# Strassen's seven products for the first two gate/up blocks, one step per token quarter

## The chip, the cores and the metric

The kernel runs on one NeuronCore of a Trainium2 chip. TensorE (PE) multiplies matrices; VectorE (DVE), ScalarE (ACT) and GpSimd (POOL) do elementwise work; SyncE (SP) issues most transfers. Each engine has its own instruction stream, which it executes in order, and semaphores tie the streams together. The metric is the device time of one execution in microseconds (us).

## The reference, cut to what matters

1024 prompt tokens and 64 sample tokens, model width 1024, fp32, one layer:

```python
h = rmsnorm(x, g_mix); z = h @ w_in                    # 1024 -> 5 * 512
b_gate, c_gate, v, glu_val, glu_gate = split(z, 5)
y_a = b_gate * dwconv3(c_gate * v)
y_b = silu(layernorm(dwconv31(glu_val * sigmoid(glu_gate)) + bias))
x = x + concat(y_a, y_b) @ w_out                       # "out projection"
h2 = rmsnorm(x, g_ffn)                                 # "second norm"
x = x + (silu(h2 @ w_gate) * (h2 @ w_up)) @ w_down     # d_ff = 2816 = 22 blocks of 128
y = rmsnorm(x, g_final)
```

The sample tokens have their own convolution histories, and the new histories are outputs too.

## The kernel before, in words

Activations stand transposed, channels on partitions, tokens along the columns. The 1088 columns are two halves of 544, and four pieces of 272. A *quarter* `s` (0 or 1) here is the piece `s` of each half, so 2 x 272 columns (`quarter`). Every matmul is 128x128 by 272 columns, in fp16. An fp32 product is made of three of them: each operand is split into a high fp16 part (a copy on ACT, `high`, L312) and a low one (the rest, on DVE, `low`, L315), and high x high, high x low and low x high are added in PSUM (`products`, L299). Weights are split the same way when they are loaded (`split_w`, L275 on ACT and L276 on DVE), into eight slots of 512 columns (`whl`), or, if an entry is marked resident, into a tile of its own.

From the third block on, gate and up of a block are one Strassen step. The weights of the block form a 2x2 (rows of the model's halves, columns gate and up), the operands another (B11, B12, B21, B22: half of the model width by half of the tokens), and seven products replace eight (`SEVEN`). They need sums of weights (S1 to S4, on POOL, L501 to L512) and differences of operands (T1 to T4, on DVE). The first two blocks are plain (`plain_task`): for each quarter, block, and gate or up, one task of 8 x 3 x 2 = 48 matmuls. They run while the operands of the Strassen steps come to be: quarter 0's norm (`second_norm`) during quarter 1's out projection, its differences (`combinations`) from that one's end on, and quarter 1's both during the plain tasks.

What sets the order is a list of tasks, written out in program order (`run_tasks`). A task is one group of matmuls, what reads its banks (`post`), and some steps of background work (`bg`): the layer norm, the second norm or the differences, each a generator of which a `Stream` takes so many steps. At the start of a task the low halves that were left over are issued (`flush`, over the list `late`), and up to two weight tiles are prepared (`fill_one`), at most 12 tasks ahead and only while one of the eight slots is free; a resident one only from the out projection on. Each engine's queue follows that order. Column sums of a norm go to PE in the middle of another task, at a share of its matmuls (`midway`, PART1 to PART3). Accumulators are pairs of PSUM banks, three of them in this stage, taken in turn (`bank2`). Small scratch tiles (`small`) are a pool of eleven.

The out projection runs quarter 0 (L1103 adds its result to x), then quarter 1. For quarter 0 its first three blocks are each cut in two: part a takes the terms of the first three channel blocks, part b the rest. Those three blocks' weights are split again for quarter 1.

Transfers of weights go through two tiles `wf` of 1 MB on SP's queue; preparing the first entry of a load issues the next load, which waits until the tile's last reader is done.

After the plain tasks `begin_strassen` cuts the banks anew and hands the operands of blocks 0 and 1 for the down product to `late`, where each waits a number of turns (`delayed`).

Of the kernel before, what the change touches and what calls it, by code (L numbers as in the profile page):

```python
# [132 lines left out]
NPART, NBEG = 3, 3  # L133

ORDER1 = (*range(NPART, KB), *range(NPART))
LASTG = len(GROUPS) - 1
# [26 lines left out]
def trunk(ctx, tc, x, par, sta, stb, w_in, w_o, w_gu, w_ds, w_dl, y, st_out):  # L163
# [60 lines left out]
    def bank2():  # L224
        k = psum["turns"][psum["n"] % len(psum["turns"])]
        psum["n"] += 1
# [56 lines left out]
    def products(outs, terms, first=True, last=True, part=(0, None), low_last=None):  # L283
# [3 lines left out]
        if low_last:  # L287
            todo.sort(key=lambda a: a[1] == low_last)
        one, end = todo[0], todo[-1]
        todo = todo[slice(*part)]  # L290
# [112 lines left out]
    for s, b in [(0, b) for b in range(KB)] + [(1, b) for b in ORDER1]:  # L403
        if b >= NPART and s:
            W_O[s, b] = W_O[0, b]
            continue
        if b % 2 == 0 or s and b == NPART:
            raws.append((w_o[b // 2], 2048, s == 0 and b < 2 * (NPART // 2 + 1)))
        r, o, e = len(raws) - 1, (b % 2) * 1024, len(entries)
        if b < NPART:  # L410
            W_O[s, b] = [(e + q, 0) for q in range(2)]
            entries += [dict(raw=r, off=o + WS * q, n=WS) for q in range(2)]
        else:
            W_O[s, b] = [(e, q * WS) for q in range(2)]
            entries.append(dict(raw=r, off=o, n=1024, resident=True))
    W_GU, W_DN = {}, {}

    def gate_up_entries(n):
        W_GU[n] = len(entries)
        if n < NE:  # L420
            entries.extend(dict(raw=len(raws), off=WS * q, n=WS) for q in range(4))
        else:
            entries.extend(dict(raw=len(raws), strassen=a[0], n=WS) for a in SEVEN)
        raws.append((w_gu[n], 2048, False))

# [11 lines left out]
    for n in range(GROUPS[0][1]):  # L437
        gate_up_entries(n)
# [24 lines left out]
    def prepare(i):  # L463
# [15 lines left out]
        if name is None:  # L479
            o, n = e["off"], e["n"]  # L480
            return split_w(raw[:, o : o + n], e.get("resident") and unit_v, raws[r][2])
# [17 lines left out]
        if name == "S1":  # L499
# [3 lines left out]
            sums["S2"] = s2  # L503
            src = s1
        elif name == "S2":
            src = sums["S2"]
# [3 lines left out]
        elif name == "S4":  # L510
            src = sums["S2"]
# [21 lines left out]
    def fill_one(t, first=None):  # L533
# [5 lines left out]
        if res and t < marks["out"] or not res and len(live) == NSLOT:  # L539
            return False  # L540
# [441 lines left out]
    def b_post(acc, j, hf):  # L982
# [9 lines left out]

        return rest
# [78 lines left out]
    def out_task(b, s, *bg, part=None):  # L1072
        ws = W_O[s, b]

        def terms(ks):
            out = []
            for k in ks:
                w, col = ws[k // NJ]
                t = (ya + yb)[k]
                out.append((whl[w], col + (k % NJ) * P, [(t, s * CW), (t, HT + s * CW)]))  # L1080
            return out

        def emit_a():
            keep["out", b] = bank2()
            pair_products(keep["out", b], terms(range(NBEG)), last=False)

        def emit_b():
            while s not in ln_done:
                flush()
                ln(1)  # L1090
            flush()
            acc = keep.pop(("out", b))
            pair_products(acc, terms(range(NBEG, KB)), first=False)
            return acc

        def emit():
            acc = bank2()
            pair_products(acc, terms(range(KB)))
# [7 lines left out]
        w = sorted({w for w, _ in ws})  # L1106
        if part == "a":
            add(w[:1], emit_a, lambda _: None, *bg)
        elif part == "b":
            add(w, emit_b, post, *bg)  # L1110
        else:
            add(w, emit, post, *bg)

    ssum, rstd2 = {}, {}
# [794 lines left out]
```

## Time and profile before

| | |
|---|---|
| median of 3 runs | 1001.45 us (1001.19 to 1001.87) |
| profiled execution | 1001.27 us |
| its span, first to last instruction | 999.5 us |
| granted TensorE clock | 0.999 |
| PE, DVE, ACT, POOL busy | 987.7, 721.9, 421.5, 358.0 us |
| matmuls | 8664 |

A row of a timeline reads: start, duration, engine, line of the kernel, operation, what is written <- what is read, shapes, count, and in brackets how long the engine was idle before it and what ended that. A matmul's duration contains its pipeline, so the pace is read from the distance of starts. In a row of stages each engine has its busy time and, in brackets, its instructions; then come the granted clock (1.00 is full), the share of the transfer engines and GB/s.

### The profile page before, as it was taken

To read this page: it belongs to the slowest core of one execution; us is meant where nothing else is said; L and a number is where in the kernel's file an instruction comes from. 1 tells how busy PE (TensorE), PEld (TensorE's weight loads), DVE (VectorE), ACT (ScalarE), POOL (GpSimd) and SP (SyncE) were. 2 spreads that over 40 slices of the span, in tenths; PEclk is the share of its full clock that TensorE was granted. 3 is DMA by queue.
4 is the path that set the end of the run, shared out by engine and by line. 5 is a ranking of instruction groups with operands and counts; after the bars stand their busy time and mean duration, and the time that the engine had idled before them with its cause. 6 is when DMAs were issued, how large, how long until landed. Compare 5 with 4: busy or idle time off the path is not lost.

```text
span 999.5 us, 20038 instructions
## 1 busy us (share of the span) xinstructions
PE 987.7 (99%) x8664; PEld 835.9 (84%) x8664; DVE 721.9 (72%) x1009; ACT 421.5 (42%) x742; POOL 358.0 (36%) x295
## 2 busy tenths in 40 slices
PE   8999999999999999999999999999999999999997
PEld 8888888888888888888888888888888888888886
DVE  6959999987676778866665665666566556676586
ACT  6512243247452534644223444422345443244455
POOL 1947986656000204232134212213422221363044
PEclk9999999999999999999999999999999999999999
DMA  9300111111500111120112112111211201131105
GB/s 341 110 19 25 61 44 54 43 43 58 209 1 1 43 43 44 43 74 33 65 43 85 43 43 75 33 64 43 86 44 43 75 33 64 65 127 43 43 2 179
DMA packets 18568, 64.61 MB, mean 65 GB/s; under 512 B 1296, under 2 KB 9632, under 8 KB 13616
## 3 DMA queue, kind: packets, MB, share of 16 engines
q1 hardware_dynamic: 18160, 63.12, 18.1%
q8 instruction: 67, 1.10, 0.4%
q14 instruction: 21, 0.17, 0.1%
q10 hardware_dynamic: 272, 0.13, 0.0%
q0 software_dynamic: 48, 0.09, 0.0%
HBM read 58.28 MB, written 5.05 MB: 63 GB/s over the span
## 4 chain that ended last, share of the span: by engine, by line
PE 76%; DVE 19%; issue 2%; ACT 2%; POOL 1%; DMA 1%; DVEq 0%; SPq 0%; ACTq 0%; POOLq 0%
PE two L299 69%; DVE cv L641 12%; PE one L817 3%; PE one L1651 1%; DVE u L315 1%; DVE whl L276 1%; PE one L299 1%; PE stat L324 1%; DVE v L1167 1%; PE two L1651 1%; DMA u<-w_in 1%; DVE cv L636 1%; DVE s L985 0%; DVE u L956 0%; ACT h L312 0%
## 5 line engine op out<-in xcount | busy, mean ns | idle before, releaser
L299 PEld LDWEIGHTS <-whl 128*128 128x128 f16 x7182 | 702.7, 98 | 131.7 <-issue 2.2
L299 PE MATMUL two<-u,whl 128*128 128x272 f16 x4416 | 523.3, 279 | 0.5 <-DVE u L315 0.3
L299 PE MATMUL two<-h,whl 128*128 128x272 f16 x2736 | 329.5, 279 | 0.8 <-DVE s L985 0.6
L512 POOL TENSOR_TENSOR s<-wf,s 128x512 f32<-128x512 f32 (+1 forms) x32 | 37.7, 1177 | 397.9 <-DVE whl L276 397.9
L641 DVE SCALAR_TENSOR_TENSOR cv<-u,par_t,cv 128x1024 f32<-128x1024 f32 x108 | 130.6, 1303 | 0.1
L1373 DVE SCALAR_TENSOR_TENSOR s<-two,s 128x544 f32<-128x544 f32 x60 | 43.5, 724 | 108.9 <-PE two L299 108.9
L276 DVE SCALAR_TENSOR_TENSOR whl<-wf,whl 128x512 f16<-128x512 f32 (+1 forms) x150 | 116.3, 781 | 3.8 <-ACT whl L275 3.8
L275 ACT ACTIVATE whl<-wf 128x512 f16<-128x512 f32 (+1 forms) x150 | 87.1, 586 | 73.1 <-PE two L299 71.6
L1487 DVE SCALAR_TENSOR_TENSOR xt<-two,xt 128x544 f32<-128x544 f32 x84 | 60.8, 724 | 55.9 <-PE two L299 55.6
L275 ACT ACTIVATE whl<-s 128x512 f16<-128x512 f32 (+1 forms) x96 | 56.1, 584 | 67.1 <-PE two L299 60.9
L276 DVE SCALAR_TENSOR_TENSOR whl<-s,whl 128x512 f16<-128x512 f32 (+1 forms) x96 | 62.2, 652 | 19.9 <-ACT whl L275 19.5
L501 POOL TENSOR_TENSOR s<-wf 128x512 f32<-128x512 f32 (+1 forms) x32 | 39.4, 1232 | 93.7 <-DVE s L356 91.7
L299 PE MATMUL two<-u,v 128*128 128x272 f16 x480 | 56.3, 279 | 0.0
L312 ACT ACTIVATE h<-s 128x544 f16<-128x544 f32 (+2 forms) x62 | 37.9, 623 | 40.3 <-DVE s L1416 11.4
L1369 ACT ACTIVATE s<-two 128x544 f32<-128x544 f32 x60 | 36.9, 614 | 42.8 <-PE two L299 42.6
L299 PEld LDWEIGHTS <-v 128*128 128x128 f16 x480 | 47.0, 98 | 9.0
L274 POOL TENSOR_TENSOR whl<-wf,whl 128x512 f16<-128x512 f32 x38 | 46.9, 1259 | 10.1 <-ACT whl L273 10.1
L817 PE MATMUL one<-h,u 128*128 128x272 f16 (+2 forms) x480 | 46.1, 256 | 1.0 <-ACT h L312 1.0
L817 PEld LDWEIGHTS <-u 128*128 128x128 f16 x480 | 39.9, 98 | 7.2 <-issue 1.4
L508 POOL TENSOR_TENSOR wf<-wf 128x512 f32<-128x512 f32 (+1 forms) x32 | 43.8, 1369 | 0.0
L315 DVE TENSOR_TENSOR h<-s,h 128x544 f16<-128x544 f32 (+2 forms) x61 | 40.6, 687 | 3.0 <-ACT h L312 1.9
L502 POOL TENSOR_TENSOR s<-s,wf 128x512 f32<-128x512 f32 (+1 forms) x32 | 41.4, 1294 | 2.5
(167 smaller groups left out, 801.8 us busy)
## 6 DMA issues: line engine op xcount, KB each, us to landing
wf<-w_gu SPq DMA_DIRECT2D x22, 1024.0 KB, 4.9
wf<-w_ds SPq DMA_DIRECT2D x12, 768.0 KB, 4.1
wf<-w_in SPq DMA_DIRECT2D x8, 1024.0 KB, 5.1
wf<-w_o SPq DMA_DIRECT2D x6, 1024.0 KB, 5.0
xt<-x SPq DMA_DIRECT2D x3, 1088.0 KB, 12.5
y<-xt SPq DMA_DIRECT2D x4, 544.0 KB, 3.4
u<-w_in SPq DMA_DIRECT2D x4, 512.0 KB, 7.5
wf<-w_dl SPq DMA_DIRECT2D x2, 1024.0 KB, 4.9
```

Source lines behind the costliest of these rows:

```text
L274: return whl, lambda: gps.tensor_tensor(lo, wf, hi, ALU.subtract) and None
L275: act.activation(hi, wf, AF.Copy, scale=WSC)
L276: return whl, lambda: dve.scalar_tensor_tensor(lo, wf, WSC, hi, ALU.mult, ALU.subtract) and None
L299: pe.matmul(out, w_[:, wpart, col : col + P], hl[:, apart, t0 : t0 + out.shape[1]], start=first and (i, q) == one, stop=last and (i, q) == ...
L315: eng.tensor_tensor(lo, tmp, hi, ALU.subtract)
L501: gps.tensor_tensor(s1, a21, a22, ALU.add)
L502: gps.tensor_tensor(s2, s1, a11, ALU.subtract)
L508: gps.tensor_tensor(a21, a11, a21, ALU.subtract)
L641: dve.scalar_tensor_tensor(o_, i_, w, c, ALU.mult, ALU.add)
L817: pe.matmul(accs[c, i][:, o : o + cw], w4[i][:, wpart, k * P : (k + 1) * P], h[k][:, apart, t0 : t0 + cw], start=len(done) == 1, stop=len( ...
L1373: dve.scalar_tensor_tensor(o, src, IN_SC, o, ALU.mult, ALU.add)
L1487: dve.scalar_tensor_tensor(o, bk[a_][:, :, :CW], IN_SC, o, ALU.mult, ALU.add)
```

## The change

Blocks 0 and 1 become Strassen steps too, both in one task, one token quarter at a time: seven tasks per quarter, each of 2 blocks x 12 matmuls of one 272-column piece (`duo_tasks`). The order of the seven products differs between the quarters (`DUO`); in quarter 1 the last product has a bank of its own and is joined by DVE. The results are kept by half, both blocks in one tile (`gate`).

The second norm makes operands per quarter, each name in a tile of its own, in the order in which the products use them (`FORMS`), with the differences made in place. B12, which no product uses, is not made. `STEPS0` and `DUO_STEPS` say how many steps run in each task: all of quarter 0's run in quarter 1's out projection.

The weights of the two blocks are prepared in the order of use, block 0 and 1 in turn: A11 and A12 as one resident tile of 1024 columns, S1 and S2 resident, S3, S4 and A22 in slots. `since` says from which task after the out projection's start a resident entry may be prepared. Both blocks' loads stay in `wf` until A22 is split.

The out projection is no longer cut: eight tasks per quarter. Block 0 takes the fourth channel block last (`K_FIRST`), and that one's last low half is issued at once. The weights of its first three blocks stay in six slots for quarter 1. The layer norm's steps for quarter 1 begin in the first out task and not in the fourth.

The down product's operands of blocks 0 and 1 wait 5, 10, 15 and 20 turns in `late` (`BEHIND`), not 0, 3, 6 and 9.

```diff
-NPART, NBEG = 3, 3
+NPART = 3
 ORDER1 = (*range(NPART, KB), *range(NPART))
+FORMS = ("T1 T2 B21 T3 B22 T4".split(), "T1 B21 T2 B22 T3 T4".split())
+K_FIRST = 0, 1, 2, 4, 5, 6, 7, 3
+BEHIND = 5
+STEPS0 = (1, 2, 2, 2, 2, 3, 3, 100)
+DUO = ("A11 S1 S2 A12 S3 S4 A22", "A11 S1 A12 S2 S4 S3 A22")
+DUO_STEPS = ((1, 0, 2, 2, 2, 1, 2), (1, 2, 2, 2, 2, 100, 0))
...
+    def bank2(k=None):
+        if k is None:
+            k = psum["turns"][psum["n"] % len(psum["turns"])]
+            psum["n"] += 1
...
-    def products(outs, terms, first=True, last=True, part=(0, None), low_last=None):
...
         for n, (i, q) in enumerate(todo):
-            for part_, fn in list(midway):
+            for part_, fn in list(midway) if beside else ():
...
-    for s, b in [(0, b) for b in range(KB)] + [(1, b) for b in ORDER1]:
...
-        if b % 2 == 0 or s and b == NPART:
-            raws.append((w_o[b // 2], 2048, s == 0 and b < 2 * (NPART // 2 + 1)))
+    for b in range(KB):
+        if b % 2 == 0:
+            raws.append((w_o[b // 2], 2048, b < 2 * (NPART // 2 + 1)))
...
+    def first_pair_entries():
+        r = len(raws)
+        raws.extend((w_gu[n], 2048, False) for n in range(NE))
+        W_GU.update((n, {}) for n in range(NE))
+        for what, since in (("A", 5), ("S1", 9), ("S2", 9), ("S3", 0), ("S4", 0), ("A22", 0)):
+            for n in range(NE):
+                e = len(entries)
+                if what == "A":
+                    W_GU[n].update(A11=(e, 0), A12=(e, WS))
+                    entries.append(dict(raw=r + n, off=0, n=2 * WS, resident=n, since=since + n))
+                    continue
+                W_GU[n][what] = e, 0
+                entries.append(dict(raw=r + n, strassen=what, n=WS))
+                if what in ("S1", "S2"):
+                    entries[-1].update(resident=n, since=since)
...
+            home = None
+            if "resident" in e:
+                home = unit if e["resident"] is not True and e["resident"] == 0 else unit_v
...
+        if "resident" in e:
+            if name == "S1":
+                sums["two", r] = unit_v([P, 2, 2, n], F16)
+            return split_w(src, lambda *_: sums["two", r][:, "S1 S2".split().index(name)])
         return split_w(src)
...
-        if res and t < marks["out"] or not res and len(live) == NSLOT:
+        if res and t < marks["out"] + entries[i].get("since", 0):
+            return False
+        if not res and len(live) == NSLOT:
             return False
...
+        if (j, hf) == (NJ - 1, 1):
+            return rest()
         return rest
...
-    def out_task(b, s, *bg, part=None):
...
+        def emit():
+            assert s in ln_done
+            acc = bank2()
+            terms = []
+            for k in K_FIRST if b == 0 else range(KB):
...
+                terms.append((whl[w], col + (k % NJ) * P, [(t, s * CW), (t, HT + s * CW)]))
+            pair_products(acc, terms)
             return acc
...
-        w = sorted({w for w, _ in ws})
-        if part == "a":
-            add(w[:1], emit_a, lambda _: None, *bg)
-        elif part == "b":
-            add(w, emit_b, post, *bg)
...
+    def operand(name, kp, s):
+        return ops[name, s].rearrange("p a k c -> p a (k c)"), kp * CW
...
+        tq, ts, pend = {}, {}, []
+        def settle(n):
+            while len(pend) > n:
+                low(*pend.pop(0))
+        def put(name, u, t):
+            if (name, s) not in ops:
+                ops[name, s] = unit([P, 2, 4, CW], F16)
+            o = ops[name, s][:, :, 2 * u : 2 * u + 2]
+            high(o[:, 0], t)
+            pend.append((o[:, 1], t, o[:, 0]))
+            settle(1)
+        def norm(u, q):
+            new = unit if (s, u, q) == (0, 0, 0) else single_v if (u, q) == (1, 1) else unit_v
+            t = tq[u, q] = new([P, 2, 2, CW])
+            for kk in range(2):
+                k = 4 * q + 2 * u + kk
+                dve.scalar_tensor_tensor(
+                    t[:, kk], quarter(xt[:, k], s), prm(PG2 + k), r, ALU.mult, ALU.mult
+                )
+        def form(name, u):
+            if name[0] == "B":
+                t = tq[u, int(name[1]) - 1][:, :, int(name[2]) - 1]
+            else:
+                b11, b12, b21, b22 = (tq.get((u, q), tq[u, 0])[:, :, i] for q in (0, 1) for i in (0, 1))
+                if name == "T1":
+                    ts[u] = halves(small())
+                a, b, t = {
+                    "T1": (b12, b11, ts[u]),
+                    "T2": (b22, ts[u], ts[u]),
+                    "T3": (b22, b12, b12),
+                    "T4": (b21, ts[u], ts[u]),
+                }[name]
+                dve.tensor_tensor(t, a, b, ALU.subtract)
+            put(name, u, t)
...
+            norm(u, 0)
+            form("B11", u)
+            yield
+        for name in FORMS[s]:
+            for u in range(2):
+                if name == FORMS[s][1]:
+                    norm(u, 1)
+                    yield
+            for u in range(2):
+                form(name, u)
                 yield
         settle(0)
         yield
...
-    def plain_task(n, q, s, *bg):
...
+    def copied(src):
+        o = halves(small())
+        act.activation(o, src, AF.Copy, scale=IN_SC)
+        return o
+    def joined(src, o):
+        dve.scalar_tensor_tensor(o, src, IN_SC, o, ALU.mult, ALU.add)
+        return o
+    def duo_tasks(s):
+        bk = {}
+        order = DUO[s].split()
+        chained = order[-2] != "S3"
+        seven = {w_: (b_, a_) for w_, b_, a_ in SEVEN}
+        if not chained:
+            seven["A22"] = "T4", "W"
+        homes = {"Y": "ab"[s], "Z": "a", "W": "ba"[s]}
+        def gate(hf, src, by, sg):
+            if hf not in fu:
+                fu[hf] = unit([P, NE, HT])
+            o = fu[hf][:, :, s * CW : (s + 1) * CW]
+            dve.scalar_tensor_tensor(o, src, by, sg, ALU.mult, ALU.mult)
+        def task(i):
+            name = order[i]
+            b_, a_ = seven[name]
+            fresh = a_ not in [seven[w_][1] for w_ in order[:i]] or not chained and name == "A22"
+            final = a_ not in [seven[w_][1] for w_ in order[i + 1 :]] or not chained and name == "A12"
+            def emit():
+                if a_ not in bk:
+                    bk[a_] = bank2(homes[a_])
+                for n in range(NE):
+                    w, col = W_GU[n][name]
+                    terms = [
+                        (whl[w], col + kp * P, [operand(b_, kp, s)]) for kp in range(4)
+                    ]
+                    products([bk[a_][:, n, :CW]], terms, fresh, final, beside=n == 1)
+            def post(_):
+                acc = bk[a_][:, :, :CW]
+                if name == "A11":
+                    bk["c11"] = copied(acc)
+                elif name == "S1":
+                    bk["c22"] = copied(acc)
+                elif name == "S2":
+                    bk["c12"] = copied(acc)
+                elif name == "A12":
+                    sg = joined(acc, bk["c11"])
+                    act.activation(sg, sg, AF.Silu)
+                elif name == "S3":
+                    joined(acc, bk["c22"])
+                    if not chained:
+                        bk["c21"] = copied(acc)
+                elif name == "S4":
+                    sg = joined(acc, bk["c12"])
+                    act.activation(sg, sg, AF.Silu)
+                elif chained:
+                    gate(0, acc, 1.0 / WSC, bk["c11"])
+                else:
+                    gate(0, joined(acc, bk["c21"]), ASC, bk["c11"])
+                if name == order[5]:
+                    return lambda: gate(1, bk["c22"], ASC, bk["c12"])
+            add([W_GU[n][name][0] for n in range(NE)], emit, post, lambda: step_on(s, i))
+        for i in range(7):
+            task(i)
+    def step_on(s, i):
+        if s == 0 and i == 0:
+            sn[0](100)
+        sn[1](DUO_STEPS[s][i])
...
-                    return f_done(n, hf, fu[n][:, hf * HT : (hf + 1) * HT])
-                late.append(lambda k=3 * (2 * n + 1 - hf), fn=start: delayed(k, fn))
+                    return f_done(n, hf, fu[hf][:, n])
+                late.append(lambda k=BEHIND * (2 * n + 2 - hf), fn=start: delayed(k, fn))
...
-                    hl, c0 = operand(b_, kp)
-                    terms.append((whl[w], kp * P, [(hl, c0), (hl, c0 + CW)]))
+                    terms.append((whl[w], kp * P, [operand(b_, kp, s) for s in range(2)]))
...
-    comb = [Stream(combinations(s)) for s in range(2)]
...
-    for b in range(NPART):
-        out_task(b, 0, lambda: ln(1) if 0 not in ln_done else None, part="a")
...
         def bg(b=b):
-            if b >= NPART:
-                ln(1 if b < KB - 1 else 100)
+            ln(1 if b < KB - 1 else 100)
...
-        out_task(b, 0, bg, part="b" if b < NPART else None)
+        out_task(b, 0, bg)
...
+        out_task(b, 1, lambda i=i: sn[0](STEPS0[i]))
     for s in range(2):
-        for n in range(NE):
...
-                plain_task(n, q, s, bg)
+        duo_tasks(s)
```

More of the change, by code (lines that the diff above doesn't have):

```diff
@@ L436, in trunk @@
     aside = set()
-    for n in range(GROUPS[0][1]):
+    first_pair_entries()
+    for n in range(NE, GROUPS[0][1]):
         gate_up_entries(n)
@@ L510, in prepare @@
         elif name == "S4":
-            src = sums["S2"]
+            src = sums["S2", r]
             gps.tensor_tensor(src, a12, src, ALU.subtract)
```

142 lines of the change are left out of this document (12 added, 130 removed).

## The prediction

> **What bounds the kernel now.** I read the busy shares and the chain that ended last first.
>
> ```profile
> span 999.5 us, 20038 instructions
> PE 987.7 (99%) x8664; PEld 835.9 (84%) x8664; DVE 721.9 (72%) x1009; ACT 421.5 (42%) x742; POOL 358.0 (36%) x295
> PE 76%; DVE 19%; issue 2%; ACT 2%; POOL 1%; DMA 1%; DVEq 0%; SPq 0%; ACTq 0%; POOLq 0%
> ```
>
> PE is busy all the time and 76% of the chain is its own. The DVE part of the chain is early (the taps) and around the stage that the change rewrites, so the second view is the stages there: the out projection of quarter 1 (first row), the plain gate/up blocks (second), the first Strassen block (third).
>
> ```profile
> core 0: us, PE busy (x) PEld busy (x) DVE busy (x) ACT busy (x) POOL busy (x), PEclk, DMA share, GB/s
> 296.20:335.10 38.90, 38.90 (x338) 32.86 (x337) 27.42 (x41) 14.29 (x24) 0.00 (x0) 1.00 0.01 1
> 335.10:381.40 46.30, 45.88 (x391) 38.30 (x389) 36.13 (x55) 20.51 (x34) 7.50 (x5) 1.00 0.13 46
> 381.40:400.00 18.60, 18.60 (x163) 15.70 (x162) 15.88 (x18) 8.05 (x15) 9.97 (x7) 1.00 0.16 58
> ```
>
> The clock is full (1.00), PE has no gap to speak of, and DVE runs at 70%, 78% and 85%. So matmuls taken out are time taken out, as long as DVE, which makes the operands, keeps up. Third view, the timeline of PE, then of DVE, in that stage:
>
> ```profile
> 295.57 22.87 PE L299 MATMUL two<-u,v 128*128 128x272 f16 x196
> 318.27 21.94 PE L299 MATMUL two<-u,whl 128*128 128x272 f16 x188
> ...
> 340.31 0.76 PEld L324 LDWEIGHTS stat<-s,ones 128*128 128x128 f32 x4 [0.39 <-DVE s L356]
> 340.31 1.18 PE L324 MATMUL stat<-s,ones 128*128 128x272 f32 x4
> 341.33 19.04 PE L299 MATMUL two<-u,whl 128*128 128x272 f16 x163
> 360.69 59.54 PE L299 MATMUL two<-u,whl 128*128 128x272 f16 x510 [0.32 <-DVE u L315]
> ...
> 960.06 4.33 PE L299 MATMUL one<-h,u 128*128 128x272 f16 x36
> 964.23 2.25 PE L299 MATMUL one<-h,whl 128*128 128x272 f16 x18
> ```
>
> From 295.57 to 318.27, 196 matmuls take 22.70 us: 0.1158 us each. In the last two rows, where a weight tile serves one matmul and not two, 36 take 4.17 us: 0.1158 again. PE waits for DVE twice: 0.39 us ahead of the column sums, 0.32 us for a low half.
>
> ```profile
> 329.59 0.73 DVE L1103 SCALAR_TENSOR_TENSOR xt<-two,xt 128x544 f32<-128x544 f32 x1 [2.06 <-PE two L299]
> 330.23 0.72 DVE L1188 TENSOR_TENSOR s<-v,s 128x544 f32<-128x544 f32 x1
> 330.86 0.72 DVE L315 TENSOR_TENSOR u<-s,u 128x544 f16<-128x544 f32 x1
> ...
> 335.15 0.72 DVE L1103 SCALAR_TENSOR_TENSOR xt<-two,xt 128x544 f32<-128x544 f32 x1 [0.46 <-PE two L299]
> ...
> 338.33 1.29 DVE L276 SCALAR_TENSOR_TENSOR whl<-wf,whl 128x512 f16<-128x512 f32 x2
> 339.53 0.72 DVE L356 TENSOR_TENSOR s<-s,s 128x544 f32<-128x544 f32 x1
> ...
> 381.39 0.72 DVE L1336 SCALAR_TENSOR_TENSOR u<-two,s 128x544 f32<-128x544 f32 x1 [1.64 <-PE two L299]
> ```
>
> The rows at 335.15 and 381.39 start on PE's last matmul of the out projection and of the plain blocks: the stage lasts 46.24 us. Tasks of 48 matmuls are 5.56 us apart (329.59, 335.15). One DVE instruction of 544 columns follows another after 0.64 us; the low half of a 512-column weight tile takes 0.60.
>
> **The change, part by part.** *Strassen for blocks 0 and 1.* Plain: 8 tasks of 48 matmuls = 384. Strassen: 2 quarters x 7 products x 2 blocks x 12 = 336. Each at 0.1158, and the column sums at 0.92 (a distance below): the stage should be 384 x 0.1158 + 0.92 = 45.39 and is 46.24, so 0.85 us of it is waiting. The new one without waits is 336 x 0.1158 + 0.92 = 39.83 us: 6.41 less than now, 5.56 of it matmuls. PE's weight loads stay one per matmul and shorter than it.
>
> *DVE's account.* I count from the end of the out projection (0). Norms and newton steps from these rows:
>
> ```profile
> 294.65 1.08 PE L324 MATMUL stat<-s,ones 128*128 128x272 f32 x4
> 295.57 22.87 PE L299 MATMUL two<-u,v 128*128 128x272 f16 x196
> ...
> 296.87 0.72 DVE L344 SCALAR_TENSOR_TENSOR stat<-stat,s 128x544 f32<-128x544 f32 x1
> 299.16 1.47 DVE L1167 SCALAR_TENSOR_TENSOR u<-xt,par_t,stat 128x544 f32<-128x544 f32 x2
> ...
> 302.43 1.47 DVE L1167 SCALAR_TENSOR_TENSOR v<-xt,par_t,stat 128x544 f32<-128x544 f32 x2
> 303.81 1.35 DVE L315 TENSOR_TENSOR u<-u,u 128x544 f16<-128x544 f32 x2
> ...
> 341.59 0.62 ACT L341 ACTIVATE s<-stat 128x544 f32<-128x544 f32 x1 [2.02 <-PE stat L324]
> 342.23 1.28 ACT L1333 ACT_TABLE_LOAD   x1
> 343.52 0.62 ACT L1333 ACTIVATE s<-two 128x544 f32<-128x544 f32 x1
> ```
>
> Three newton steps are 2.29, a pair of norms 1.38. Quarter 0's combinations all move into the out projection: per task xt and the square's add 1.28, plus 1.9 to 3.8 of norms, differences and low halves, plus 1.2 for two weight tiles: 3.8 to 5.2 us of each 5.56. They fit, barely; nothing on PE waits until the queue is over a task late, as there are three pairs of banks. If that cover goes, the lateness arrives at the column sums.
>
> There, DVE has xt, T4's last difference, two low halves, two weight tiles and the add: 6 x 0.64 + 1.2, with 0.15 for a copy on ACT about 5 at worst, 4.7 as I lay it out; PE gets there at 47 matmuls, 5.44. Slack 0.5 to 0.7, where today PE waits 0.39. The sums end at 6.4, the root on ACT at 7.1, newton at 9.4. Then in order of use, with the joins and gates between them (0.64 each): B11's low halves by 15.3 (PE wants them at 20.4), T1's by 21.9 (23.2), B21's by 25.2 (25.9), T2's by 27.1 (28.7), B22's by 30.7 (31.5), T3's by 33.2 (34.3), T4's by 35.8 (37.1). Every operand is early, but by 0.7 to 1.6 us; DVE is busy some 34 of 39.8 us, 86%. ACT's table load (1.28), today right behind the root, comes ahead of quarter 0's first silu and holds T1's copies to 15.9 and 16.5, just as DVE asks for them. The bank that quarter 0's last product leaves is read at 23.3, while the second quarter asks for one at 23.2: 0.1. So I bound the new waits by 0 and by the 0.85 of today for a likely course, and take 0.4.
>
> *Weights.* The four splits per block become an unsplit pair (1024 wide), and S1, S2, S3, S4, A22; six re-made splits of the out weights and their two 1 MB loads go. DVE loses 6 + 8 low halves of 0.60 and gets ten, and two wide ones:
>
> ```profile
> 249.21 2.35 DVE L276 SCALAR_TENSOR_TENSOR v<-wf,v 128x1024 f16<-128x1024 f32 x2
> ```
>
> 8.4 us against 6.0 + 2.4, the same. SP's load of block 2 now waits until block 0's A22 is split, at 3.4:
>
> ```profile
> wf<-w_gu SPq DMA_DIRECT2D x22, 1024.0 KB, 4.9
> ```
>
> It lands at 8.3; ACT wants it at 7.6 and holds only a copy behind it until B11's high half at 10.8. On SP only block 3's load is queued behind. Cost 0; if it were 3 us later ACT's copies would follow, still ahead of 20.4.
>
> *Out projection without its split first three blocks, layer norm three tasks sooner, last low half at once.* PE's work is the same. Block 0 wants ya3 after 42 matmuls, 4.9 us in; its low half, behind one DVE instruction and one copy of 0.64, is done some 2 us in. Where layer norm's second half runs today, PE has no gap:
>
> ```profile
> 268.00:296.20 28.20, 28.20 (x234) 23.54 (x233) 18.79 (x29) 16.67 (x23) 0.00 (x0) 1.00 0.11 38
> ```
>
> So a sooner one gains 0; it loses at most what one blocked DVE instruction costs (1.7, below), as its chain from sums to sums is the same. I take 0.
>
> *POOL.* S1 to S4 of two blocks are eight more instructions. What one costs DVE:
>
> ```profile
> 340.39 2.90 POOL L501 TENSOR_TENSOR s<-wf 128x512 f32<-128x512 f32 x1 [91.68 <-DVE s L356]
> ...
> 344.59 1.27 POOL L508 TENSOR_TENSOR wf<-wf 128x512 f32<-128x512 f32 x1
> 344.72 1.71 DVE L315 TENSOR_TENSOR u<-s,u 128x544 f16<-128x544 f32 x1 [2.56 <-ACT u L312]
> ...
> 395.99 1.72 POOL L508 TENSOR_TENSOR wf<-wf 128x512 f32<-128x512 f32 x1
> 396.50 0.71 DVE L1373 SCALAR_TENSOR_TENSOR s<-two,s 128x544 f32<-128x544 f32 x1
> ```
>
> A low half that meets one takes 1.71 for 0.72, so 1.0 us is lost; an instruction that reads a PSUM bank (L1373) loses nothing. Six of the eight need only block 0's and 1's loads and a free scratch tile, and POOL is idle: they should run in the middle of the first out quarter, where DVE has gaps. Block 2's three meet newton and norms, which read PSUM. So I take 0, with 12 x 1.0 as the upper bound.
>
> This split by operand is also what the Trainium skill says (SBUF — State Buffer, "Who interferes with whom"): a VectorE instruction with two SBUF inputs contends with a GpSimd one that reads SBUF, and the later one blocks fully. The trace agrees (1.71 against 0.71). By that rule alone all low halves and differences that overlap would pay, which is the second rival.
>
> *Blocks 0 and 1's operands for the down product* come up to 20 queue turns later, not 9. The third row of stages (85% DVE) gets lighter at first: 0, as PE waits for nothing there today.
>
> **Sum.** The profiled execution took 1001.27 us, 1.8 around its span, against a median of 1001.45. 1001.27 - 6.41 + 0.4 = 995.3.
>
> **Rivals.** *First, DVE sets the pace in the new stage.* If block 2's three POOL instructions meet low halves (3 x 1.0) and two copies on ACT are exposed (0.6 each, like the silu above), T1 and B21 are 4.2 late against 0.7 of slack: 3.5 of waits, 998.4. For it: 86% with slacks under 2 us. Against: what is late once is then early for the rest, as PE moves back too.
>
> *Second, slower: POOL's port.* All twelve POOL instructions fall between the last out tasks and quarter 1's T1, and each holds a two-input DVE instruction up by 1.0: 12 - 0.7 = 11.3 us, 1006.2. It decides from the eighth on, when 6.41 + 0.7 is used up. For it: today POOL waited 91.7 us for a scratch tile until 340.39, just there. Against: the scratch tiles which the eight get were freed tasks earlier.
>
> *Third, no gain: weights late.* Six of eight slots are held to the end of the stage, so block 2 begins with two tiles. Were two of its tasks 2.78 us late each, 5.56 is lost: 1000.4. For it: DVE at 85% there. Against: the third tile is asked for five tasks after the first slot is freed.
>
> **How the numbers follow.** Forecast 0.62 (994.5 to 996.5), first rival 0.21 (to 999.3), third 0.09, second 0.08. A measurement of this kernel tells about 0.2%, 2 us, from no change. Faster by more takes the forecast and nearly all of the first: 0.82; same 0.10; slower 0.08. Low is 994.86 less the scatter of the runs, 994.5; reaching into the first rival until some 8 in 10 are held gives 998.6.
>
> **What would show it.** Right: 48 matmuls fewer, the stage near 40 us, PE's wait ahead of the sums gone, waits on low halves together under 1 us, POOL's new rows before the last out tasks. Wrong: a PE wait of over 1 us on L315 or on a gate, DVE rows of 1.7 us in a row ahead of it, or PE waiting for weight tiles in block 2.

## The result, and the profile after

The changed kernel takes 995.49 us (median of 6 executions, 994.87 to 995.70), the kernel before, in the same session, 1001.32 us (1000.68 to 1002.10). The ratio is 0.9940, with a 95% interval of 0.9928 to 0.9953. It is faster by 5.8 us, or 0.6%, and the forecast was 995.3 us. One later execution of the changed kernel took 1282.6 us at a mean clock of 0.752 and is left out of its median below. The page of the changed kernel, in the rows that answer to those of before:

```profile
span 993.7 us, 19954 instructions
PE 982.2 (99%) x8616; PEld 831.8 (84%) x8616; DVE 729.7 (73%) x1010; ACT 423.3 (43%) x743; POOL 369.8 (37%) x303
PE 78%; DVE 16%; issue 2%; ACT 1%; POOL 1%; DMA 1%; DVEq 0%; SPq 0%; ACTq 0%; POOLq 0%
```

There are 48 matmuls fewer, PE's busy time is down by 5.5 us and the span by 5.8. DVE and POOL have 8 and 12 us more to do, and it does not show in PE's time. The timeline of PE through the new stage (line numbers are those of the changed kernel; L309 is `products`):

```profile
318.20 16.84 PE L309 MATMUL two<-u,whl 128*128 128x272 f16 x144
334.88 1.55 PE L309 MATMUL two<-u,u 128*128 128x272 f16 x12
336.27 4.22 PE L309 MATMUL two<-u,v 128*128 128x272 f16 x35
340.33 1.08 PE L334 MATMUL stat<-s,ones 128*128 128x272 f32 x4
...
346.92 5.72 PE L309 MATMUL two<-u,whl 128*128 128x272 f16 x48
353.31 2.94 PE L309 MATMUL two<-u,whl 128*128 128x272 f16 x24 [0.67 <-DVE s L1335]
...
363.04 4.33 PE L309 MATMUL two<-u,v 128*128 128x272 f16 x36
367.21 73.02 PE L309 MATMUL two<-u,whl 128*128 128x272 f16 x629
```

The stage begins at 334.88 with A11 of block 0. Quarter 1's last three products begin at 367.21, and with 72 matmuls of 0.1158 they end at 375.55: 40.67 us, against 46.24 before. Without waits it would be 39.83, so 0.84 is waiting. That is what it was before (0.85), at another place: the waits for the column sums and for a low half are gone, and there is one ahead of the 24 matmuls of quarter 0's A22. The row's 0.67 counts from the modelled end of the last matmul; by the distance of starts it is 353.31 - (346.92 + 48 x 0.1158) = 0.83, which is all the waiting that the stage has. What PE waits for stands on DVE:

```profile
342.16 0.73 DVE L354 SCALAR_TENSOR_TENSOR stat<-stat,s 128x544 f32<-128x544 f32 x1 [2.19 <-ACT s L351]
...
344.46 2.86 DVE L1175 SCALAR_TENSOR_TENSOR v<-xt,par_t,stat 128x544 f32<-128x544 f32 x4
347.24 1.01 DVE L325 TENSOR_TENSOR u<-v,u 128x544 f16<-128x544 f32 x1
...
351.31 0.71 DVE L325 TENSOR_TENSOR u<-s,u 128x544 f16<-128x544 f32 x1
351.94 0.68 DVE L289 SCALAR_TENSOR_TENSOR whl<-s,whl 128x512 f16<-128x512 f32 x1
352.55 0.71 DVE L1335 SCALAR_TENSOR_TENSOR s<-two,s 128x544 f32<-128x544 f32 x1
353.18 2.84 DVE L1175 SCALAR_TENSOR_TENSOR v<-xt,par_t,stat 128x544 f32<-128x544 f32 x4
```

From 342.16 on DVE has no gap: newton, four norms, a low half, weights, the join of A12 (348.77), T1's steps, weights, and at 352.55 the join that reads S3's sum out of its bank pair (L1335, `joined`). In quarter 0, A11, S2, S3 and A22 all add up in that one pair, so A22 may not write there before the join has read it. POOL's new instructions ran here:

```profile
266.67 1.28 POOL L526 TENSOR_TENSOR s<-wf 128x512 f32<-128x512 f32 x1 [18.09 <-DMA wf<-w_gu]
...
277.98 3.47 POOL L533 TENSOR_TENSOR wf<-wf 128x512 f32<-128x512 f32 x2
311.54 3.52 POOL L537 TENSOR_TENSOR s<-wf,s 128x512 f32<-128x512 f32 x2 [30.09 <-DVE v L289]
343.81 1.27 POOL L526 TENSOR_TENSOR s<-wf 128x512 f32<-128x512 f32 x1 [28.74 <-DVE stat L355]
```

Six of the eight are in the first out quarter, two (S4) in the second; block 2's three come at 343.81, beside newton and the norms.

### The profile page after: what moved, and what is told of

It reads as the page before. It is cut to its first block, busy times and chain, and to the rows that moved or that the text cites. A ratio compares the mean times of both kernels' runs of the same rounds, so it can differ in the third digit from the quotient of the medians.

```text
span 993.7 us, 19954 instructions
## 1 busy us (share of the span) xinstructions
PE 982.2 (99%) x8616; PEld 831.8 (84%) x8616; DVE 729.7 (73%) x1010; ACT 423.3 (43%) x743; POOL 369.8 (37%) x303
## 4 chain that ended last, share of the span: by engine, by line
PE 78%; DVE 16%; issue 2%; ACT 1%; POOL 1%; DMA 1%; DVEq 0%; SPq 0%; ACTq 0%; POOLq 0%
PE two L309 72%; DVE cv L672 12%; PE one L848 3%; PE one L1680 1%; PE one L309 1%; PE two L1680 1%; PE stat L334 1%; DVE cv L667 1%; DMA u<-w_in 1%; DVE s L1016 0%; DVE u L987 0%; DVE whl L289 0%; ACT h L322 0%; DVE u L650 0%; DVE v L1175 0%
## 5 line engine op out<-in xcount | busy, mean ns | idle before, releaser
L309 PEld LDWEIGHTS <-whl 128*128 128x128 f16 x6942 | 679.2, 98 | 127.5 <-issue 2.2
L309 PE MATMUL two<-u,whl 128*128 128x272 f16 x4176 | 495.8, 279 | 0.7 <-DVE s L1335 0.7
L309 PE MATMUL two<-h,whl 128*128 128x272 f16 x2736 | 329.5, 279 | 0.8 <-DVE s L1016 0.6
L537 POOL TENSOR_TENSOR s<-wf,s 128x512 f32<-128x512 f32 (+1 forms) x34 | 41.3, 1216 | 420.5 <-DVE whl L289 390.4
L1335 DVE SCALAR_TENSOR_TENSOR s<-two,s 128x544 f32<-128x544 f32 x67 | 48.5, 723 | 109.9 <-PE two L309 109.8
L289 DVE SCALAR_TENSOR_TENSOR whl<-wf,whl 128x512 f16<-128x512 f32 (+1 forms) x140 | 112.4, 806 | 2.5 <-ACT whl L288 2.5
L288 ACT ACTIVATE whl<-wf 128x512 f16<-128x512 f32 (+1 forms) x140 | 81.5, 584 | 72.4 <-PE two L309 71.3
L309 PE MATMUL two<-u,v 128*128 128x272 f16 x624 | 73.4, 279 | 0.0
L309 PEld LDWEIGHTS <-v 128*128 128x128 f16 x624 | 61.1, 98 | 11.5
L1331 ACT ACTIVATE s<-two 128x544 f32<-128x544 f32 x67 | 41.2, 615 | 46.1 <-PE two L309 44.8
L848 PE MATMUL one<-h,u 128*128 128x272 f16 (+2 forms) x480 | 45.9, 256 | 1.3 <-ACT h L322 1.3
L527 POOL TENSOR_TENSOR s<-s,wf 128x512 f32<-128x512 f32 (+1 forms) x34 | 45.5, 1338 | 2.7
L848 PEld LDWEIGHTS <-u 128*128 128x128 f16 x480 | 39.9, 98 | 7.2 <-issue 1.7
```

Source lines behind the costliest of these rows:

```text
L288: act.activation(hi, wf, AF.Copy, scale=WSC)
L289: return whl, lambda: dve.scalar_tensor_tensor(lo, wf, WSC, hi, ALU.mult, ALU.subtract) and None
L309: pe.matmul(out, w_[:, wpart, col : col + P], hl[:, apart, t0 : t0 + out.shape[1]], start=first and (i, q) == one, stop=last and (i, q) == ...
L527: gps.tensor_tensor(s2, s1, a11, ALU.subtract)
L848: pe.matmul(accs[c, i][:, o : o + cw], w4[i][:, wpart, k * P : (k + 1) * P], h[k][:, apart, t0 : t0 + cw], start=len(done) == 1, stop=len( ...
L1331: act.activation(o, src, AF.Copy, scale=IN_SC)
```

## The experiments

Each is the changed kernel with one edit, the last with two. Two things were to be told apart: whether the gain is the matmuls less that one wait, or DVE's pace with matmuls that are not the limit; and which parts of the change, counted at nothing, are worth nothing.

### The matmuls put back

```diff
-                    products([bk[a_][:, n, :CW]], terms, fresh, final, beside=n == 1)
+                    for _ in range(2 if name == "A12" else 1):
+                        products([bk[a_][:, n, :CW]], terms, fresh, final, beside=n == 1)
```

> The product A12 of blocks 0 and 1 is computed twice into its bank in each quarter (the second starts the bank anew): 48 matmuls come back, nothing else changes. Theory: the gain is the 48 matmuls less a wait of 0.67 us ahead of quarter 0's last product, where DVE's join after S3 is late. 48 x 0.1158 = 5.56 come back, and the 1.4 us of PE work which now stand ahead of that product in its quarter (12 matmuls x 2 blocks x 0.1158 = 2.78, between A12 and S3) give DVE time to make the join, so the wait goes: +5.56 - 0.67 = +4.9, about 1000.4 us against 995.5. Rival, DVE paces the stage and PE's matmuls there are not the limit: the added work fills time that is waiting already, below +3 us.

Measured: 1000.63 us, 5.1 above the changed kernel. From A11 of block 1 to quarter 1's last three products it is 35.67 us in its trace for 30.94, 4.7 more. Quarter 0's S3, S4 and A22, in PE's timeline of this kernel, run as one row:

```profile
349.06 8.50 PE L309 MATMUL two<-u,whl 128*128 128x272 f16 x72
```

The wait is gone, as DVE had 2.8 us more for the join, and 5.56 - 0.67 = 4.9 was expected. PE's matmuls are the limit in this stage.

### Another bank for quarter 0's last product

```diff
-FORMS = ("T1 T2 B21 T3 B22 T4".split(), ...
+FORMS = ("T1 T2 B21 B22 T3 T4".split(), ...
-DUO = ("A11 S1 S2 A12 S3 S4 A22", ...
+DUO = ("A11 S1 S2 A12 S4 S3 A22", ...
-        homes = {"Y": "ab"[s], "Z": "a", "W": "ba"[s]}
+        homes = {"Y": "a", "Z": "a", "W": "b"}
```

> Quarter 0 takes quarter 1's way: S4 before S3, and the last product (A22) in the bank pair that A12 left, joined by DVE, instead of adding on to the bank that S3 has just left to be read. Quarter 1's first bank changes place with its third. Theory: PE's wait of 0.67 us ahead of quarter 0's last product is for the bank, which DVE's join still has to read; with another bank it is gone, and one more DVE instruction (0.64) makes quarter 1's operands 0.6 later, inside their slack: no wait over 0.3 us left in the stage, 0.4 to 0.7 us faster than the changed kernel, about 995.0. Rival: the product waits for its operand T4 or its weights, and the bank is a coincidence: a wait of about 0.7 stays in that place, 995.5 or above.

Measured: 994.93 us. In its timeline quarter 0's last three products run without a gap:

```profile
347.30 8.50 PE L309 MATMUL two<-u,whl 128*128 128x272 f16 x72
355.64 1.55 PE L309 MATMUL two<-u,u 128*128 128x272 f16 x12
```

DVE has one more instruction there and PE does not wait for it. The edit changes the order of S3 and S4 too; the next run leaves the order as it is.

### The joins first

```diff
-DUO_STEPS = ((1, 0, 2, 2, 2, 1, 2), ...
+DUO_STEPS = ((1, 0, 2, 0, 4, 1, 2), ...
```

> The two steps of quarter 1's second norm that make T1 are taken one task later, behind the join of S3 (steps per task 1, 0, 2, 0, 4, 1, 2 for 1, 0, 2, 2, 2, 1, 2). DVE's work is the same. Theory: the joins of A12 and S3 come 2.5 us sooner, the wait of 0.67 us is gone, T1's low halves are 0.3 us later than now and still ahead of PE (22.2 against 23.2 us after the out projection's end): about 995.0. Rival: DVE has no slack left, and what is taken from the joins is missing at T1 or at the gate: a wait of 0.5 to 2 us on a low half (L325) or a gate (L1352), 995.4 to 997.

Measured: 994.07 us. From A11 of block 1 to quarter 1's last three products (336.27 to 367.21 in the changed kernel: 30.94 us) it takes 30.10 (335.86 to 365.96), which is 252 matmuls at 0.1158 and the sums' 0.92: no waiting left. With the run before, that shows that it was the bank. The join has moved up to 349.72, ahead of T1:

```profile
348.49 0.71 DVE L1335 SCALAR_TENSOR_TENSOR s<-two,s 128x544 f32<-128x544 f32 x1
349.12 0.68 DVE L289 SCALAR_TENSOR_TENSOR whl<-s,whl 128x512 f16<-128x512 f32 x1
349.72 0.71 DVE L1335 SCALAR_TENSOR_TENSOR s<-two,s 128x544 f32<-128x544 f32 x1
350.36 0.71 DVE L1192 TENSOR_TENSOR s<-v 128x544 f32<-128x544 f32 x1
```

As the gain was larger than the wait, it was run once more, beside the changed kernel on one chip.

> The changed kernel as it is, on the same chip as the next two, to compare them with it: 995.5 us (994.9 to 995.7 so far), a wait of 0.7 to 0.9 us on L1335 ahead of quarter 0's last product.

> T1's two steps behind the join of S3, as above, now beside the changed kernel. Theory: what it gains is the wait for the bank, 0.7 to 0.9 us, and nothing else: 994.7 if the changed kernel takes 995.5, and no wait of PE in the new stage. Rival: the 1.4 us by which its median was lower than the changed kernel's is its own: 994.1 again, with something shorter than in the changed kernel that is not that wait.

Measured: 995.70 us (four executions) and 994.62. Against the kernel before that is 0.9942 (0.9928 to 0.9956) and 0.9929 (0.9916 to 0.9943). The difference is 1.1 us. From A11 of block 1 to quarter 1's last three products it is 31.10 us in the one trace (336.11 to 367.21) and 30.10 in the other (337.24 to 367.34): 1.0 us, the whole of the wait, which is 0.83 in the row and 0.99 by the distance of starts. The two profiled executions do not differ in their times (995.47 and 995.59), because the second reached this stage 1.1 us later; PE's first waits for ACT (L848) were 1.1 us in the one and 1.9 in the other. This version is the fastest of all that ran, though its interval overlaps that of the changed kernel.

### The last low half late again

```diff
-        if (j, hf) == (NJ - 1, 1):
-            return rest()
```

> The last low half of the fourth channel block (ya3) goes back into the list of what is issued at the next task's start; the order of the terms in the first out task stays. Theory: it then stands behind the three sums of the layer norm on DVE, one of which meets a POOL instruction (2.54 us for 0.72 in the changed kernel), and ends some 6.7 us after the last projection, while PE wants it after 42 matmuls, 4.9 us: a wait of about 1.9 us on L325, 997.4. Rival, as the prediction's step had it with slack to spare: PE has other terms to do and nothing is seen, 995.5.

Measured: 996.37 us, 0.9 above. DVE and PE of this kernel, where the first out task asks for ya3:

```profile
246.50 2.42 POOL L287 TENSOR_TENSOR v<-wf,v 128x1024 f16<-128x1024 f32 x1 [2.93 <-ACT v L286]
246.85 2.65 DVE L325 TENSOR_TENSOR u<-s,u 128x544 f16<-128x544 f32 x1
...
249.56 5.61 PE L309 MATMUL two<-u,whl 128*128 128x272 f16 x47 [0.73 <-DVE u L325]
```

The place was right, the size not: the POOL instruction meets the low half and not one of the sums, and it is done at 249.5. By the distance of starts PE loses 249.56 - (243.45 + 45 x 0.1158) = 0.9 us there, so the part that issues it at once is worth that.

### POOL's sums left out

```diff
+    first_raws = set()
...
+        first_raws.update((r, r + 1))
...
-        if name == "S1":
+        if isinstance(W_GU.get(0), dict) and r in first_raws and name[0] == "S":
+            src = {"S1": a21, "S2": a22, "S3": a21, "S4": a12}[name]
+        elif name == "S1":
```

> Leaves out POOL's eight instructions for blocks 0 and 1: S1 to S4 of those two blocks are replaced by quarters of the weights as they are, so these blocks' results are other numbers; splits, products and transfers are unchanged. Theory: the eight cost nothing, as six run in the first out quarter and two in the second where DVE has gaps: within 0.3 us of 995.5, though DVE rows of 1.7 us disappear. Rival, POOL's port: each costs DVE about 1.0 us that reaches PE: up to the whole wait of 0.67 us goes, 994.8, or more where DVE's lateness is hidden elsewhere.

Measured: 995.67 us, and the wait ahead of A22 is 0.80. The eight instructions cost nothing where they are.

### The layer norm's second half as late as before

```diff
-            ln(1 if b < KB - 1 else 100)
+            if b >= 3:
+                ln(1 if b < KB - 1 else 100)
```

> The layer norm's steps for quarter 1 begin in the fourth out task again, as in the kernel before. Theory: a sooner second half gains nothing by itself, PE had no gap there: within 0.3 us of 995.5. Rival: in the changed kernel its work would meet the new weights' splits (two of 1024 columns) and POOL's six instructions between 266 and 281 us, and quarter 1's out projection would wait for its operands: a wait of 0.5 to 3 us on a low half or on the column sums near 280 to 296 us, 996 to 998.5.

Measured: 997.05 us, 1.6 above. The rival was right. DVE, PE and POOL of this kernel:

```profile
275.30 2.65 DVE L366 TENSOR_TENSOR s<-s,s 128x544 f32<-128x544 f32 x2
...
276.11 1.26 POOL L526 TENSOR_TENSOR s<-wf 128x512 f32<-128x512 f32 x1 [27.20 <-DVE s L366]
...
278.10 1.16 PE L334 MATMUL stat<-s,ones 128*128 128x272 f32 x4 [0.86 <-DVE s L366]
```

S1 of block 0 meets the additions of the layer norm's squares, two of which take 2.65 us for 1.35, and PE waits 0.86 us for their column sums. By the distance of starts that costs 1.0 us, and A22 waits 0.2 longer (0.90 in its row), so these stages account for 1.2 of the 1.6. Another 0.3 the profiled execution had lost before them (the matmuls that begin at 213.54 in the changed kernel begin at 213.86).

### The down product's operands as early as before

```diff
-                late.append(lambda k=BEHIND * (2 * n + 2 - hf), fn=start: delayed(k, fn))
+                late.append(lambda k=3 * (2 * n + 1 - hf), fn=start: delayed(k, fn))
```

> Blocks 0 and 1's operands for the down product are made after 0, 3, 6 and 9 turns as before, not 5 to 20. Theory (the prediction's step at cost 0): DVE's queue is longer in blocks 2 and 3, but nothing that PE needs is late: within 0.3 us of 995.5. Rival: from 373 to 384 us DVE already runs without a gap in the changed kernel, and four or five more instructions ahead of the weights of block 2 and its joins make PE wait 0.5 to 3 us on a weight tile or on L1335 there: 996 to 998.5.

Measured: 996.18 us (995.03 to 996.52), 0.7 above. PE's list of waits shows no new one, but its stages do. The first row of stages is this kernel's, the second the changed kernel's:

```profile
400.00:440.00 40.00, 39.87 (x345) 33.54 (x344) 31.36 (x45) 20.91 (x37) 10.93 (x8) 1.00 0.21 72
400.00:440.00 40.00, 40.00 (x348) 33.80 (x346) 32.46 (x47) 21.95 (x39) 10.82 (x8) 1.00 0.16 55
```

PE is idle for 0.13 us here and for none there, and by the distance of starts it loses 0.3: the 912 matmuls from quarter 1's last three products on take 105.93 us in this kernel and 105.64 in the changed one. By the chain that ended last, PE waits at 401.4 for ACT's copy out of a bank. The kernel before has the same wait, also 0.3 us by the distance of starts and some 25 us behind the stage's end; two pieces of its chain (start, duration, what):

```profile
405.95 0.52 ACT s L1369
406.52 539.49 PE two L299 x4656
```

So the longer wait in `late` is worth 0.3 us, and the rival was right in kind, though it put the wait at 0.5 or more. The profiled execution is 0.9 above the changed kernel's: 0.45 of it lies ahead of the stage, 0.16 at A22 and 0.29 here.

### Quarter 0's norm late

```diff
-STEPS0 = (1, 2, 2, 2, 2, 3, 3, 100)
+STEPS0 = (1, 1, 1, 1, 1, 1, 1, 1)
```

> Quarter 0's norm goes one step per out task, so its last nine steps (nine low halves and four differences, 8.3 us of DVE) all come behind the first product of the new stage instead of in the out projection. Theory: DVE's account of the stage sets when PE waits, and the bank that quarter 0's last product adds to is the first to be late: the column sums' steps begin 5.0 us later, the join of S3 ends 22.9 us after the out projection's end where PE wants it at 17.7: a wait of about 5.1 us on L1335 in place of 0.67, +4.4, 999.9 us. Rival, only operands count: T1's second low half is ready at 27 and wanted at 23.9, a wait of 3.1 on L325, 998.0. Rival, PE is not touched: 995.5.

Measured: 1003.85 us, 8.4 above, slower than the kernel before (ratio 1.0026, 1.0015 to 1.0036). All three expectations were too low. PE's timeline, and then four stages of it:

```profile
351.79 8.24 PE L309 MATMUL two<-u,whl 128*128 128x272 f16 x48 [4.96 <-ACT s L1331]
361.28 2.94 PE L309 MATMUL two<-u,whl 128*128 128x272 f16 x24 [1.25 <-DVE s L1335]
```

```profile
core 0: us, PE busy (x) PEld busy (x) DVE busy (x) ACT busy (x) POOL busy (x), PEclk, DMA share, GB/s
351.70:354.00 2.30, 2.21 (x10) 1.47 (x10) 2.23 (x4) 0.04 (x1) 0.00 (x0) 0.50 0.00 0
354.00:356.00 2.00, 2.00 (x10) 1.37 (x9) 2.00 (x4) 1.12 (x2) 0.00 (x0) 0.50 0.00 0
356.00:358.00 2.00, 2.00 (x15) 1.51 (x13) 2.00 (x5) 1.98 (x3) 0.00 (x0) 0.76 0.00 0
358.00:360.00 2.00, 2.00 (x18) 1.57 (x16) 2.00 (x5) 1.88 (x4) 0.00 (x0) 1.00 0.00 0
```

It is the same bank pair, one reader sooner: S3 waits 4.96 us for ACT's copy of S2's sum (L1331), which stands in ACT's queue behind the high halves of T4, and those wait for DVE, two of whose instructions there met block 2's POOL sums (344.23 and 345.94: 1.79 and 1.78 us for 0.72). Then PE's clock is at 0.50, and 48 matmuls take 8.24 us and not 5.72 as in the changed kernel. By the distance of starts S3 begins 5.1 us late (351.79 for 346.66), its matmuls take 2.5 longer, and A22 waits 0.6 longer (1.25 for 0.67): 8.2.

### A smaller lateness

```diff
-STEPS0 = (1, 2, 2, 2, 2, 3, 3, 100)
+STEPS0 = (1, 2, 2, 2, 1, 1, 1, 1)
```

> Steps per out task 1, 2, 2, 2, 1, 1, 1, 1 instead of all ones: of quarter 0's norm six steps (six low halves, three differences, 5.7 us of DVE) come behind the first product of the new stage, not nine steps (8.3 us). With nine, PE waited 4.96 us for ACT's copy of S2's bank, which stood behind the high halves of T4, then 1.25 us for the join, and its next 48 matmuls took 8.24 us at a granted clock of 0.50, 0.76 and 1.00. Theory: the wait for the copy shrinks by the 2.6 us of DVE that are gone, to 2.4, the wait for the join stays near 1.2, and the clock stays at 1.00 because PE is idle too short for it to fall: 995.5 + 2.4 + 1.2 - 0.7 = 998.4 us. By the Trainium skill (TensorE: Matmul & The Clock Gate, The HAM clock gate) the clock halves after an idle window of about 3.4 us, which says the same. Rival: the clock falls after any wait of some 2 us, or for another reason than the wait: 2.7 us more, about 1001.

Measured: 1002.37 us. The wait for the copy is 0.33, but PE waits 5.76 us for the join, and the clock falls there:

```profile
341.97 1.30 POOL L526 TENSOR_TENSOR s<-wf 128x512 f32<-128x512 f32 x1 [27.66 <-DMA wf<-w_gu]
342.07 1.79 DVE L1192 TENSOR_TENSOR s<-v,s 128x544 f32<-128x544 f32 x1
...
343.35 1.64 POOL L527 TENSOR_TENSOR s<-s,wf 128x512 f32<-128x512 f32 x1
...
343.78 3.51 DVE L325 TENSOR_TENSOR u<-s,u 128x544 f16<-128x544 f32 x2
...
358.13 4.64 PE L309 MATMUL two<-u,whl 128*128 128x272 f16 x24 [5.76 <-DVE s L1335]
362.60 1.55 PE L309 MATMUL two<-u,u 128*128 128x272 f16 x12
```

```profile
355.00:357.00 2.00, 0.00 (x0) 0.00 (x0) 2.00 (x4) 1.74 (x3) 0.00 (x0) 0.50 0.00 0
```

Two things were not in the expectation. Block 2's POOL instructions now meet two-input instructions (1.79 and 3.51 us for 0.72 and 1.36), and the 24 matmuls of A22 take 358.13 to 362.60, 4.47 us for 2.78. The last run takes the first away.

```diff
+    second_raws = set()
...
+        second_raws.add(r + 2)
...
-        if name == "S1":
+        if r in second_raws and name[0] == "S":
+            src = {"S1": a21, "S2": a22, "S3": a21, "S4": a12}[name]
+        elif name == "S1":
```

> The run before, with POOL's four instructions for block 2 left out: its sums of weights are replaced by quarters of the weights, so block 2's results are other numbers; all else is the same. In the run before, three of the four met two-input DVE instructions of quarter 0's T4 and low halves: one of 1.79 us and two that took 3.51, for 0.72 each, so 3.2 us lost, and PE waited 5.76 us for the join and then ran 24 matmuls in 4.47 us for 2.78 at a clock of 0.50. Theory (POOL's port, and a clock that falls only after a wait as long as that one): DVE's join ends 3.2 us sooner, PE waits 2.6, the clock stays at 1.00: 1002.4 - 3.2 - 1.7 = 997.5 us. Rival, the long DVE rows are due to their own order (a low half waiting for ACT's copy): nothing changes, 1002.4. Rival, the clock falls also at 2.6 us of waiting: 999.2.

Measured: 999.79 us. DVE's long rows are short, and the stages of PE behind the wait:

```profile
343.30 0.72 DVE L1196 TENSOR_TENSOR s<-v,s 128x544 f32<-128x544 f32 x1
343.94 1.53 DVE L325 TENSOR_TENSOR u<-s,u 128x544 f16<-128x544 f32 x2
...
356.31 4.61 PE L309 MATMUL two<-u,whl 128*128 128x272 f16 x24 [3.19 <-DVE s L1339]
```

```profile
353.00:355.00 2.00, 0.12 (x2) 0.00 (x0) 2.00 (x5) 1.91 (x4) 0.00 (x0) 1.00 0.00 0
355.00:357.00 2.00, 0.69 (x4) 0.51 (x4) 2.00 (x5) 0.00 (x1) 0.00 (x0) 0.86 0.00 0
357.00:360.00 3.00, 3.00 (x16) 1.95 (x15) 3.00 (x5) 0.31 (x1) 0.00 (x0) 0.53 0.00 0
```

From A11 of block 1 to A22 it is 19.56 us (336.75 to 356.31), with POOL's instructions 22.61 (335.52 to 358.13): 3.05 sooner, as the port's theory said. The clock fell also after a wait of 3.19, so the last rival was right on that in the profiled execution. Of the eleven executions, two took 997.92 and 998.04 us, near the 997.5 without a fall, at a mean clock of 0.998; the other nine took 998.7 to 1001.2, at 0.995 to 0.997. That points to a fall in those and none in the two, but only one of the eleven has its clock by stage here, and a mean of 0.997 stands in executions without such a wait too.

## Why the prediction was right

*The matmuls.* 48 x 0.1158 = 5.56 was the term that carried the sum. The stage is shorter by 5.57, and putting 48 back costs 4.7 in the trace and 5.1 by the medians, with the wait that goes. That a weight tile serves one matmul costs nothing, as the row with one output said.

*The waits.* The step that failed is the last of DVE's account, "I bound the new waits by 0 and by the 0.85 of today ..., and take 0.4": they measured 0.84, all of it in one place. The account held every operand against the time at which PE asks for it, and of the banks only the one that passes to quarter 1. It left out that A22 adds to a pair which S3's join still has to read. The prediction's own rows would have shown it: A22 is due after six products and the sums, at 6 x 2.78 + 0.92 = 17.6 us, and newton at 9.4, four norms (2.76) and the nine instructions up to the end of the join (7 x 0.64 + 2 x 0.60) make 17.8. In the trace the join was done at 18.4 (353.26). The operands came out as laid out: T1's second low half was done at 22.4 us (356.58 to 357.29, from 334.88) for 21.9. PE waited for none of them. The column sums kept some slack: their last addition ended at 339.97, and PE took them at 340.33. So today's 0.85 went and 0.84 came, and the saving inside the stage is the matmuls alone.

*Blocks 0 and 1's operands later, counted at 0.* Too low by 0.3. The prediction read that "PE waits for nothing there today" from a row of stages that ends at 400 us; the wait is at 406.5, and the longer turns in `late` take it away. With 0.84 for 0.4 and this 0.3 the sum is 1001.27 - 6.41 + 0.84 - 0.30 = 995.40, and the profiled execution took 995.44. That the forecast was as near as 0.2 us is luck in so far as these two errors have opposite signs.

*The layer norm sooner, counted at 0.* Wrong as a part of this change: PE had no gap there in the kernel before, but the change also puts S1 to S3 of two blocks into that stretch, and with the old order they cost a wait of 0.86 us. The two edits belong together; that the sooner norm gains nothing without the other was read from the kernel before and not run.

*The last low half at once.* Inside the order of terms it is worth 0.9 us; the prediction had it done in time, as it is, and gave no price for leaving it.

*POOL at 0.* Right, by the run without the eight instructions. The second rival's mechanism exists all the same: three instructions of block 2 cost DVE 3 us where they met two-input ones. In the changed kernel they meet newton and norms, which read PSUM, and a single low half loses 0.3. Behind the stage four DVE instructions between 374.81 and 381.68 lose some 3.5 us to POOL's next ones, and PE waits for none of them.

*Weights and transfers.* Block 2's load held ACT up by 1.03 us at 343.67, 8.8 us after the stage's begin; 8.3 was forecast for the landing, and nothing was late for it. No wait for a weight tile appears in blocks 2 and 3, so the third rival has nothing.

*The first rival* was the nearest: DVE does set PE's only wait there. It is 0.8 us and not 3.5: its condition, three low halves held up by block 2's POOL instructions, did not come (one lost 0.3 us), and T1 and B21 were not late.

## What to carry to other kernels

When an engine that feeds PE runs at 85%, list for each product not only when its operands are ready but when its bank has been read: a bank pair that several products add up in, with a reader after each, is a deadline for that reader's place in its queue, and moving the reader ahead of work with later deadlines cost nothing here. A list of waits can leave a short one out; the distance of starts shows it. An edit that would gain nothing alone can be what another edit needs; price it with the other one in place. Keep instructions with two SBUF inputs away from POOL's where their queue is tight, and fill that stretch with ones that read PSUM.

## What the runs showed of the hardware that was not expected

PE's clock falls after a wait of a few us. After 4.96 us of waiting it was granted at 0.50 for over 4 us and was at 1.00 again some 6 us later; after 5.76 us it was at 0.50 too; after 3.19 us it fell to 0.53 in the profiled execution, and by their times in some others and not in all. The slower matmuls behind these waits cost 1.7 us (24 matmuls, after 3.19 and 5.76) and 2.5 us (48, after 4.96) on top of the wait. The Trainium skill (TensorE: Matmul & The Clock Gate, "The HAM clock gate") has the clock halve after an idle window of about 3.4 us that runs freely and is not set off by the kernel. The trace agrees on the half clock; the wait of 3.19 us (3.35 by the distance of starts) is a little shorter than the page's window and was enough. Executions on both sides of a fall with the same kernel would fit a window that runs on its own; the window itself no run here shows.
